# A planner's durations, attention weights turned by DMA planes, and the order of one layer's projections

## The chip, the core and the metric

The kernel runs on one core of a Trainium2 chip. The core has a matrix engine (TensorE, PE in the profile, with its weight loads as PEld), a vector engine (VectorE, DVE), a scalar engine (ScalarE, ACT), a general engine (GpSimd, POOL) and a queue engine (SyncE, SP) from which nearly all DMAs are issued. Each engine executes its own instructions in the order in which they were written; semaphores make one wait for another. PE writes only to PSUM, POOL cannot read PSUM. The metric is the device time of one execution in microseconds, lower is better.

## The reference

Two layers, each a mixer and a convolutional feed-forward block, over 272 valid tokens (16 learned ones and 256 of the input) of width 1024, in float32. What matters here:

```python
def mixer(hn, ...):
    proj = hn @ w_in                          # rq rk rv rg | hq hf hi hg | dq dk dv | m0 m1 m2
    o_ret = retention(rq, rk, rv, rg)         # 4 heads
    o_hg  = hgrn2(hq, hf, hi, hg)             # 8 heads, gated linear recurrence
    o_da  = diff_attention(dq, dk, dv)        # 8 heads
    y = sum(sigmoid(m_n) * (o_n @ w_branch[n]) for n, o_n in enumerate((o_ret, o_hg, o_da)))
    return y @ w_out

def diff_attention(q, k, v, lam_p, ...):      # per head: two score maps of 64 features
    p = softmax(where(allowed, q @ k.T, MASK))
    w = p[:, :, 0] - lam * p[:, :, 1]         # the attention weights
    return rms(w @ v) * subln_g * (1 - lambda_init)

def conv_ffn(hn, ...):                        # 1024 -> 5632, three-tap convolution, silu(gate) * val, -> 1024
```

Each layer normalises its input before the mixer and before the feed-forward block, and a final normalisation ends the model.

## The kernel before

**Products.** Everything is held with features on the partitions and tokens along the free axis. Every projection is made of 128x128 weight tiles; float32 accuracy comes from splitting both operands into a rounded part and a remainder, and adding three matmuls for each tile (lines 915 to 917: high weight with high input, high with low, low with high). Weights arrive in chunks of eight tiles (`_Weights.next`, line 626): a DMA on SP into `wraw` (3 buffers), a rounding copy on ACT into `whi`, a subtraction on DVE into `wlo` (4 buffers each). These are the "main" matmuls. A pair of output tiles `(name, j)` has 16 weight tiles, 48 main matmuls.

**Stages.** `ORDER` (lines 63 to 85) is the sequence of pairs in a layer, with marks between them: `+x` makes the side work of a branch (retention `ret`, recurrence `hga`/`hgb` and its outputs `hgoa`/`hgob`, attention halves `daa`/`dab` of four heads each), `!x` says by when it is due, and `*bn` splits the finished branch n into high and low tiles for its projection `bn`. Then `wo`, 22 pairs of `fi` and the second feed-forward product `fo` follow.

**The planner.** `_Plan` collects all instructions with their operands, dependencies, buffers and a cost in microseconds, and a key, the time at which each is wanted on a clock that the main matmuls' costs advance. `_Plan.order` (line 454) then simulates the five engines: on each it takes the instruction that can start first, and among those the one with the smallest key (`rank`, line 495); a change of engine costs `CROSS` 0.4 us, a freed buffer `FREE` 0.5 us, a change of ACT's tables `SWITCH` 1.3 us, and a DMA 2.0 us beyond its cost. The order found is written out as each engine's program. The costs come from `_Engine.__getattr__` (line 580): a fixed part and a part per element for each engine, with a few exceptions by operation. Line 905 gives the cost of the three main matmuls of a tile.

**Side work in turn.** `behind` (line 1360) makes a job of a head. `in_turn` keeps the order in which the instructions of a job take buffers of one kind, and `plan.queue(ops[0], mine[-1 - apart][-1])` lets a job start only when the last instruction of the job `apart` + 1 places before it is done; for attention `apart` is 2, retention 2, otherwise 1. Buffers are few: two PSUM banks each for `main`, `bank` and `acc`, 13 `slot` tiles, four `vsrc` tiles, two each of `wts`, `two_a` and `two_b`.

**An attention head.** `da_head` (line 1274) makes the scores `ds` of both maps on PE (line 1291) in two `bank` tiles, adds the mask and takes the maxima on DVE, exponentials on ACT, and combines both maps into `w` (tile `two_a`, tokens on the partitions) with multiplications on DVE. `turn` (line 1315) then turns three 128x128 blocks of `w` by PE transposes into a third `bank` tile `wt` (line 1317), and two ACT copies bring them to `a1` (tile `wts`). POOL copies two strips of 16 columns of `w` to `dt` for `da_tail`. The product with the values, `do`, is two PE matmuls, followed by a normalisation with a POOL all-reduce (`inverse`, line 974).

**Turned values.** The values of all branches need tokens on the partitions. `to_tokens` (line 951) turns them without PE: POOL copies the lower and the upper 16 bits of the float32 words into two planes (`apart`), a DMA transpose on SP turns each (`turned`), and POOL puts them together again (`vt`).

**The folded norm.** The first four pairs behind a normalisation multiply PSUM by `rstd`; for the fifth and later ones `Norm.next` has POOL multiply `y = h * rstd`, which ACT and DVE split into `xh` and `xl`.

## Time and profile before

| what | before |
|---|---|
| three runs, us | 1304.24, 1306.25, 1305.88 (median 1305.88) |
| the profiled execution, us | 1305.7 |
| its span from first to last instruction, us | 1303.9 |
| granted TensorE clock, mean | 0.998 |
| busy: PE, DVE, ACT, POOL, us | 1285.8, 986.7, 786.7, 270.3 |
| DMA transposes | 48 |

The span is what the trace covers; the execution's own time has 1.8 us more around it. In the lines of the profile, `out<-in` names the tiles that an instruction writes and reads, `xN` how often it occurs, and the figures behind a bar are busy us, mean ns of one, and idle us of the engine before it with what ended that idleness. Line 607 is the planner's common call, so most instructions are told apart by their tiles and not by their lines. SPq is the queue part of SP; a wait is written as "who, for which tile, behind whom: us in total, times, longest".

### The profile page before, as it was taken

To read this page: it belongs to the slowest core of one execution; us is meant where nothing else is said; L and a number is where in the kernel's file an instruction comes from. 1 tells how busy PE (TensorE), PEld (TensorE's weight loads), DVE (VectorE), ACT (ScalarE), POOL (GpSimd) and SP (SyncE) were. 2 spreads that over 40 slices of the span, in tenths; PEclk is the share of its full clock that TensorE was granted. 3 is DMA by queue.
4 is the path that set the end of the run, shared out by engine and by line. 5 is a ranking of instruction groups with operands and counts; after the bars stand their busy time and mean duration, and the time that the engine had idled before them with its cause. 6 is when DMAs were issued, how large, how long until landed. Compare 5 with 4: busy or idle time off the path is not lost.

```text
span 1303.9 us, 28637 instructions
## 1 busy us (share of the span) xinstructions
PE 1285.8 (99%) x11678; PEld 1256.7 (96%) x11678; DVE 986.7 (76%) x1589; ACT 786.7 (60%) x1282; POOL 270.3 (21%) x300
## 2 busy tenths in 40 slices
PE   9999999999999999999999999999999999999998
PEld 9999989999999999999999999899999999999986
DVE  7685897798686789886575768877986867898843
ACT  6746444746576567666456474447466765776643
POOL 5021262423422020000030212634223220200000
PEclk9999999999999999999999999999999999999999
DMA  7664665643744545555555646655446446466653
GB/s 272 200 179 147 173 178 155 164 160 125 199 138 157 182 156 178 183 173 183 175 178 185 186 149 185 179 155 168 159 138 199 145 162 198 144 207 196 201 190 112
DMA packets 86868, 225.36 MB, mean 173 GB/s; under 512 B 32976, under 2 KB 33104, under 8 KB 86736
## 3 DMA queue, kind: packets, MB, share of 16 engines
q1 hardware_dynamic: 86448, 223.00, 55.3%
q8 instruction: 92, 1.51, 0.5%
q10 hardware_dynamic: 288, 0.52, 0.1%
q14 instruction: 40, 0.33, 0.1%
HBM read 216.16 MB, written 1.05 MB: 167 GB/s over the span
## 4 chain that ended last, share of the span: by engine, by line
PE 88%; DVE 9%; issue 1%; ACT 1%; DMA 0%; SPq 0%; DVEq 0%; ACTq 0%
PE main L915 26%; PE main L917 26%; PE main L916 25%; DVE wlo L607 2%; PE fo L1430 2%; PE fo L1431 2%; PE fo L1429 2%; DVE two_b L607 1%; DVE two_a L607 1%; PE lev L1107 1%; PE ds L1291 1%; PE ho L607 1%; PE ro L607 1%; PE do L607 1%; DVE two_c L607 1%
## 5 line engine op out<-in xcount | busy, mean ns | idle before, releaser
L915 PE MATMUL main<-xh,whi 128*128 128x272 f32 (+1 forms) x2368 | 682.6, 288 | 0.8 <-ACT whi L607 0.8
L917 PE MATMUL main<-xh,wlo 128*128 128x272 f32 (+1 forms) x2368 | 673.9, 285 | 1.3 <-DVE wlo L607 0.7
L916 PE MATMUL main<-xl,whi 128*128 128x272 f32 (+1 forms) x2368 | 673.3, 284 | 1.5 <-DVE xl L607 1.5
L607 DVE TENSOR_TENSOR wlo<-wraw,whi 128x1024 fp32r<-128x1024 f32 (+1 forms) x411 | 512.0, 1250 | 187.8 <-ACT whi L607 186.6
L607 ACT ACTIVATE whi<-wraw 128x1024 fp32r<-128x1024 f32 (+1 forms) x411 | 427.5, 1042 | 250.9 <-PE main L916 166.3
L917 PEld LDWEIGHTS main<-xh,wlo 128*128 128x128 f32 x2368 | 446.5, 189 | 3.1 <-DVE wlo L607 2.3
L916 PEld LDWEIGHTS main<-xl,whi 128*128 128x128 f32 x2368 | 446.6, 189 | 2.2 <-DVE xl L607 1.9
L915 PEld LDWEIGHTS main<-xh,whi 128*128 128x128 f32 x2368 | 446.7, 189 | 2.0 <-ACT whi L607 1.0
L607 POOL TENSOR_TENSOR y<-h,rstd 128x272 f32<-128x272 f32 x32 | 34.6, 1112 | 318.1 <-ACT rstd L607 318.1
L607 POOL PARTITION_ALL_REDUCE hr<-hsq x36 | 65.8, 1837 | 88.9 <-ACT hsq L607 85.9
L607 DVE SCALAR_TENSOR_TENSOR two_b<-main,small,two_b 128x256 f32<-128x256 f32 (+2 forms) x144 | 65.3, 487 | 24.4 <-ACT two_b L607 22.7
L607 POOL COPY apart<-vsrc 128x512 uint16<-128x512 uint16 x48 | 40.7, 867 | 145.2 <-ACT vsrc L607 145.0
L607 ACT ACTIVATE two_b<-main,small 128x272 f32<-128x272 f32 (+1 forms) x72 | 37.3, 566 | 23.8 <-PE main L917 22.7
L915 PE MATMUL main<-ghi,whi 128*128 128x272 f32 x176 | 51.0, 290 | 0.0
L916 PE MATMUL main<-glo,whi 128*128 128x272 f32 x176 | 50.6, 287 | 0.0
L917 PE MATMUL main<-ghi,wlo 128*128 128x272 f32 x176 | 50.3, 286 | 0.0
L607 POOL COPY vt<-turned 128x512 uint16<-128x512 uint16 x32 | 37.0, 1160 | 29.2 <-DMA turned<-apart 29.0
L915 PE MATMUL main<-b0hi,whi 128*128 128x272 f32 (+1 forms) x128 | 37.9, 296 | 0.0
L915 PE MATMUL main<-b1hi,whi 128*128 128x272 f32 (+1 forms) x128 | 37.8, 296 | 0.0
L915 PE MATMUL main<-yhi,whi 128*128 128x272 f32 (+1 forms) x128 | 36.4, 284 | 0.0
L917 PE MATMUL main<-b0hi,wlo 128*128 128x272 f32 (+1 forms) x128 | 36.4, 284 | 0.0
L917 PE MATMUL main<-yhi,wlo 128*128 128x272 f32 (+1 forms) x128 | 36.3, 284 | 0.0
(235 smaller groups left out, 1970.1 us busy)
## 6 DMA issues: line engine op xcount, KB each, us to landing
wraw<-in_w SPq DMA_DIRECT2D x402, 512.0 KB, 3.4
h<-in_h SPq DMA_DIRECT2D x4, 272.0 KB, 5.1
dec<-in_dec SPq DMA_DIRECT2D x2, 544.0 KB, 4.9
wraw<-in_w SPq DMA_DIRECT2D x4, 256.0 KB, 4.2
const<-in_const SPq DMA_DIRECT2D x1, 937.0 KB, 5.6
turned<-apart SPq DMA_TRANSPOSE x48, 4.0
gain<-in_gl SPq DMA_DIRECT2D x1, 512.0 KB, 5.1
out<-y ACTq DMA_DIRECT2D x2, 256.0 KB, 2.8
```

The costliest lines, as they stand in the source:

```text
L607: self.plan.add(self.name, lambda: f(*args, **kw), cost, outs, ins, args[2] if method == "activation" else None)
L915: nc.tensor.matmul(o, wh, hi, start=first, stop=False)
L916: nc.tensor.matmul(o, wh, lo, start=False, stop=False)
L917: nc.tensor.matmul(o, wl, hi, start=False, stop=last)
L1107: nc.tensor.matmul(o, keys, x, start=True, stop=True)
L1291: nc.tensor.matmul(ss[m][:, at : at + nk], q[half, hd, q0 : q0 + P], k[half, hd, :nk], start=True, stop=True)
L1429: nc.tensor.matmul(o, gh, wh, start=False, stop=False)
L1430: nc.tensor.matmul(o, gl, wh, start=False, stop=False)
L1431: nc.tensor.matmul(o, gh, wl, start=False, stop=end)
```

## The change

Four things change.

1. **The planner's durations.** The fixed parts of ACT and DVE become 0.2 and 0.145 us (from 0.094 and 0.068), the three main matmuls of 272 columns 0.370 us (from 0.349), and scalars, shuffles, POOL adds, POOL copies, all-reduces and DMA transposes get costs of their own. POOL is given a state: when an all-reduce follows an add or multiply of two tensors or the other way round, `RELOAD`, 8 us, is booked.
2. **The turn of the attention weights.** In `da_head` the PE transposes and the two ACT copies are replaced by the way of `to_tokens`: per head four POOL copies into `apart` (256 and 128 columns for each of the two planes), two DMA transposes of 384 columns on SP, and two POOL copies into `a1`. Their tiles come from the same four `vsrc` buffers. The helpers `planes` and `halves` move out of `to_tokens` for this.
3. **The order.** The pairs of `b0` move behind `dk` and `dv` of the second half and behind the mark `+dab`. `*b0` stays where it was.
4. **The chain of heads.** A job can start when the job before the last has done its n-th instruction from the end: for `da_head` n is 8, its last `do` matmul, otherwise 1 as before.

```diff
-    + _pairs("dq", 2, 4) + _pairs("b0", 0, 4) + _pairs("dk", 2, 4) + _pairs("dv", 2, 4)
+    + _pairs("dq", 2, 4) + _pairs("dk", 2, 4) + _pairs("dv", 2, 4)
     + [("+dab", 0)]
-    + _pairs("m1", 0, 4)
+    + _pairs("b0", 0, 4) + _pairs("m1", 0, 4)
...
+    RELOAD = 8.0
...
+            if e == "pool" and op.func is not None:
+                if op.func != code:
+                    code, t = op.func, max(t, engines[e] + self.RELOAD)
             engines[e] = t + cost
...
+            kind = args[2] if method == "activation" else None
             if self.name == "act":
                 cost += 0.093 * (len(aps) - 2) - (0.043 if ins[0].tensor.name in self.plan.psum else 0.0)
-            elif self.name == "pool" and method != "memset":
-                cost += 1.6e-3 * n
-            if method == "partition_all_reduce":
-                cost = 0.4 + 5.4e-3 * n
-            if method == "reciprocal":
+            elif method == "tensor_scalar":
+                cost += 0.065 * (len(aps) - 2) - 0.14
+            elif method in ("scalar_tensor_tensor", "stream_shuffle", "tensor_tensor_reduce"):
+                cost += 0.06
+            elif method == "reciprocal":
                 cost += 7 * self.each * n
-            elif method == "tensor_tensor_scan":
-                cost += self.each * n
+            elif self.name == "pool" and method == "tensor_tensor":
+                cost, kind = 0.55 + 2.1e-3 * n, method
+            elif self.name == "pool" and method == "tensor_copy":
+                cost = 0.35 + 1.0e-3 * n
+            elif method == "partition_all_reduce":
+                cost, kind = 0.2 + 6.3e-3 * n, method
...
             elif method == "dma_start":
-                cost = self.fixed + self.each * n * outs[0].shape[0]
+                cost = self.fixed + self.each * n * outs[0].shape[0] + (0.7 if kw.get("transpose") else 0.0)
...
-    act = _Engine(plan, nc.scalar, "act", 0.094, 0.833e-3)
-    dve = _Engine(plan, nc.vector, "dve", 0.068, 1.042e-3)
+    act = _Engine(plan, nc.scalar, "act", 0.2, 0.833e-3)
+    dve = _Engine(plan, nc.vector, "dve", 0.145, 1.052e-3)
...
-        cost = 3 * ((T - t0) / 2400 + 0.003)
+        cost = 3 * ((T - t0) / 2400 + 0.01)
...
+    def planes(name, n):
+        return new(tp, [P, 4 * T], U16, "vsrc", 4, name)[:, : 2 * n].rearrange("p (i x) -> p i x", i=2)
+
+    def halves(t):
+        return t.bitcast(U16).rearrange("p (x two) -> p x two", two=2)
...
             w = sb[0]
-            wt = bank("wt")
-
-            def turn(wt=wt, w=w):
-                for i, c in enumerate((0, P, T)):
-                    nc.tensor.transpose(wt[:, i * P : (i + 1) * P], w[:, c : c + P], ident)
-
-            plan.add("pe", turn, 0.33, [wt[:, : 3 * P]], [w[:, : T + P]])
-            act.activation(a1[:, META + P : T + P], wt[:, : 2 * P], AF.Copy)
-            act.activation(a1[:, META : META + P], wt[:, 2 * P : 3 * P], AF.Copy)
+            apart, turned = planes("apart", 3 * P), planes("turned", 3 * P)
+            for i in range(2):
+                for c, n, at in ((0, 2 * P, P), (T, P, 0)):
+                    pool.tensor_copy(apart[:, i, at : at + n], halves(w[:, c : c + n])[:, :, i])
+            for i in range(2):
+                sync.dma_start(turned[:, i].rearrange("p (b x) -> p b x", x=P), apart[:, i], transpose=True)
+            for i in range(2):
+                pool.tensor_copy(halves(a1[:, META : T + P])[:, :, i], turned[:, i])
...
-        def behind(f, until, apart=1):
+        def behind(f, until, apart=1, after=1):
...
-            mine.append(ops)
+            mine.append((ops, after))
             if len(mine) > apart:
-                plan.queue(ops[0], mine[-1 - apart][-1])
+                before, which = mine[-1 - apart]
+                plan.queue(ops[0], before[-which])
...
-            cost = 3 * (BANK / 2400 + 0.012)
+            cost = 3 * (BANK / 2400 + 0.0133)
...
                 for hd in range(4):
-                    behind(lambda: da_head(b, hd), "da", 2)
+                    behind(lambda: da_head(b, hd), "da", 2, 8)
```

More of the change, by code (lines that the diff above doesn't have):

```diff
@@ L470, in order @@
         count = 0
-        tables = "le"
+        tables, code = "le", "tensor_tensor"
         beside = False
@@ L605, in call @@
             elif method == "dma_start":
-                cost = self.fixed + self.each * n * outs[0].shape[0]
-            self.plan.add(self.name, lambda: f(*args, **kw), cost, outs, ins, args[2] if method == "activation" else None)
+                cost = self.fixed + self.each * n * outs[0].shape[0] + (0.7 if kw.get("transpose") else 0.0)
+            self.plan.add(self.name, lambda: f(*args, **kw), cost, outs, ins, kind)
         return call
@@ L949, in split @@
         tt(lo, x, hi.bitcast(F32), SUB)
+    def planes(name, n):
+        return new(tp, [P, 4 * T], U16, "vsrc", 4, name)[:, : 2 * n].rearrange("p (i x) -> p i x", i=2)
+    def halves(t):
+        return t.bitcast(U16).rearrange("p (x two) -> p x two", two=2)
     def to_tokens(src, vt, e):
-        def planes(name):
-            return new(tp, [P, 4 * T], U16, "vsrc", 4, name)[:, : 8 * P].rearrange("p (i x) -> p i x", i=2)
-        apart, turned = planes("apart"), planes("turned")
-        halves = lambda t, i: t.bitcast(U16).rearrange("p a (x two) -> p a x two", two=2)[:, :, :, i]
+        apart, turned = planes("apart", 4 * P), planes("turned", 4 * P)
         for i in range(2):
             pool.tensor_copy(apart[:, i].rearrange("p (c f x) -> p c f x", c=2, f=2),
-                             halves(src[:, :, : 2 * P], i).rearrange("p f (c x) -> p c f x", c=2))
+                             halves(src.rearrange("p f t -> p (f t)"))[:, :, i].rearrange("p (f t) -> p f t", f=2)[:, :, : 2 * P].rearrange("p f (c x) -> p c f x", c=2))
         for i in range(2):
@@ L963, in to_tokens @@
         for i in range(2):
-            pool.tensor_copy(halves(vt[:, :, e : e + 2 * P], i), turned[:, i].rearrange("p (c x) -> p c x", c=2))
+            pool.tensor_copy(vt.bitcast(U16).rearrange("p c (x two) -> p c x two", two=2)[:, :, e : e + 2 * P, i], turned[:, i].rearrange("p (c x) -> p c x", c=2))
     def tail_tokens(tails):
```

2 lines of the change are left out of this document (removed).

## The prediction

> **What bounds the kernel now.** I read the page's busy shares first, then the chain that ended last, the groups of instructions on TensorE, the waits of TensorE, and a table of busy time by stretch for the attention stages.
>
> ```profile
> span 1303.9 us, 28637 instructions
> ...
> PE 1285.8 (99%) x11678; PEld 1256.7 (96%) x11678; DVE 986.7 (76%) x1589; ACT 786.7 (60%) x1282; POOL 270.3 (21%) x300
> ...
> PE 88%; DVE 9%; issue 1%; ACT 1%; DMA 0%; SPq 0%; DVEq 0%; ACTq 0%
> ```
>
> TensorE (PE) is busy 1285.8 of 1303.9 us, and the chain that ends last is 88% PE. No stage waits for weights for long. So the time moves only by what PE no longer executes, and by the small waits at which its in-order queue stands still for another engine. The waits that the profile names, longest first:
>
> ```profile
> PE lev L1107 <- DVE hf L607: 3.2, 2, 1.7
> PE main L916 <- DVE xl L607: 1.5, 2, 1.1
> PE ho L607 <- DVE ho L607: 1.4, 2, 0.8
> PE wt L1317 <- DVE two_a L607: 1.1, 3, 0.5
> ...
> PE main L917 <- DVE wlo L607: 0.7, 3, 0.3
> PE lev L1107 <- DVE tot L607: 0.4, 1, 0.4
> PE lev L1107 <- DVE hq L607: 0.4, 1, 0.4
> ...
> PE lev L1107 <- ACT qt L607: 0.3, 1, 0.3
> ```
>
> Each is a place where the planner put a PE instruction earlier than its input was ready. Which engine is tight there is read from the stretches (columns: stretch, its length, then busy us and instruction count of PE, PEld, DVE, ACT, POOL, then the granted clock, DMA share and GB/s):
>
> ```profile
> 244.00:264.00 20.00, 20.00 (x165) 20.00 (x164) 16.26 (x19) 14.57 (x24) 15.74 (x17) 1.00 0.70 176
> 264.00:284.00 20.00, 19.19 (x156) 19.00 (x155) 19.72 (x37) 8.58 (x15) 4.15 (x3) 1.00 0.43 138
> ...
> 362.00:384.00 22.00, 22.00 (x176) 20.97 (x174) 17.91 (x43) 18.55 (x41) 8.71 (x10) 1.00 0.43 143
> ...
> 915.00:935.00 20.00, 19.43 (x164) 19.23 (x163) 19.79 (x37) 9.33 (x17) 4.28 (x4) 1.00 0.44 135
> ```
>
> DVE is at 19.72 of 20 us where the first attention half starts in layer 0 (19.79 in layer 1), and PE loses 0.8 and 0.6 us there; POOL has room in the attention stretches (4.15 of 20, 8.71 of 22) but not beside the value blocks (15.74 of 20).
>
> **Part 1, the turn leaves PE.** Each of 16 `da_head` calls (4 heads, two halves, two layers) loses three PE transposes and two ACT copies. What one turn costs PE is read from the starts around it:
>
> ```profile
> 294.04 0.28 PE L916 MATMUL main<-b0lo,whi 128*128 128x272 f32 x1
> 294.16 0.29 PE L917 MATMUL main<-b0hi,wlo 128*128 128x272 f32 x1
> 294.29 0.49 PE L1317 MATMUL wt<-const,two_a 128*128 128x128 f32 x3
> 294.54 0.37 PE L915 MATMUL main<-b0hi,whi 128*128 128x272 f32 x1
> 294.75 0.29 PE L916 MATMUL main<-b0lo,whi 128*128 128x272 f32 x1
> ...
> 296.49 0.84 PE L607 MATMUL do<-wts,vt 128*128 128x272 f32 x4
> ```
>
> Main matmuls start 0.12 us apart (294.04 to 294.16). Across the turn it is 0.38 (294.16 to 294.54), and the first one behind it takes 0.21 instead of 0.12: 0.26 + 0.09 = 0.35 us. Times 16: **-5.6 us**, all of it on the path. The bounds are -5.0, if two turns that now adjoin other side work save no switch, and -5.6.
>
> The turn's waits go with it:
>
> ```profile
> L1317 PE MATMUL wt<-const,two_a 128*128 128x128 f32 x48 | 8.9, 278 | 1.3 <-DVE two_a L607 1.1
> ...
> L1317 PEld LDWEIGHTS wt<-const,two_a 128*128 128x128 f32 x48 | 5.9, 140 | 2.5 <-DVE two_a L607 2.5
> ```
>
> The matmul row shows 1.3 us of idleness, the weight loads that come first 2.5; a wait under the 0.28 us of a pipelined matmul hides in busy time, so the two bound it from 1.3 to 3.8. I take **-2.5**, the loads' row, since it is the load that needs the weights `w`. The two ACT copies of a head go too:
>
> ```profile
> L607 ACT ACTIVATE wts<-wt x32: 258/332/403, 295.3 to 1045.3; 128x256 f32<-128x256 f32 x16, 128x128 f32<-128x128 f32 x16
> ```
>
> 32 x 0.33 = 10.6 us of an engine at 60%, behind no PE wait of the list: 0. If ACT had been late there, they would be part of the turn-to-`do` way below, which is replaced as a whole.
>
> **Part 2, the planes.** What takes the turn's place is, per head, four POOL copies (256 and 128 columns, twice), two DMA transposes of 384 columns on the SP queue, two POOL copies back. The turn-to-`do` way was 2.2 us (294.29 to 296.49). The nearest rows are the value blocks, which do the same at 512 columns:
>
> ```profile
> L607 POOL COPY apart<-vsrc x48: 611/626/1680, 74.0 to 991.6; 128x512 uint16<-128x512 uint16 x48
> ```
>
> ```profile
> L607 SPq DMA_TRANSPOSE turned<-apart x48: 1194/1197/2137, 74.7 to 993.2; - x48
> L607 POOL COPY vt<-turned x32: 767/938/1912, 77.2 to 998.1; 128x512 uint16<-128x512 uint16 x32
> ...
> DMA to landing us min/median/max: 2.4/4.0/6.0
> ```
>
> ```profile
> L607 POOL COPY apart<-vsrc 128x512 uint16<-128x512 uint16 x48 | 40.7, 867 | 145.2 <-ACT vsrc L607 145.0
> ```
>
> By columns alone the copies take 0.3 and 0.2 us when nothing is in their way, and the copies back 0.6; the page's mean of `apart`, 867 ns against the minimum of 611, adds about 0.26 each. That is 2.3 to 3.9 us of POOL per head, 37 to 62 us in all, on an engine busy 270.3 us: no bound by itself.
>
> What counts is whether `do`, the next PE instruction of the head, comes later than planned. Let S be the end of the head's last DVE multiply-add. In the new plan POOL books 0.35 us + 1 ns a column (0.61, 0.48), a transpose 1.31 us of SP and 2.0 us to land, a copy back 0.73, and every change of engine 0.4. The four copies end at S + 1.8, the second transpose follows the first at S + 3.05, lands for POOL at S + 6.75, and `do` is due at S + 7.9. On the chip, from the rows: the copies end at S + 0.45 to 1.3; the second transpose goes out 1.2 to 2.1 us behind the first (its own time on SP) and lands 4.0 us later, at S + 5.7 to 7.4; copied back in 0.6 to 0.9, S + 6.3 to 8.3. With the slowest landing (6.0) the middle of that, 7.3, becomes 9.3. A crossing costs far less than 0.4, which is what pays for this:
>
> ```profile
> 293.19 0.37 DVE L607 SCALAR_TENSOR_TENSOR two_a<-two_a,dm,two_b 128x144 f32<-128x144 f32 x1
> ...
> 293.62 0.20 POOL L607 COPY dt<-two_a 128x16 f32<-128x16 f32 x1 [0.41 <-DVE two_a L607]
> ```
>
> (293.56 to 293.62, 0.06 us.) So in the middle `do` is early by 0.6, and in the tail late by 1.4 us. Bounds: 0, and 16 x 1.4 = 22.4 us if every head is in the tail. I take **+3**, a quarter of the heads late by about 0.8, because the median landing is nearer to the early end. While PE waits at `do`, main matmuls queue behind it, so such a wait is paid in full. A POOL copy back that waits for its landing holds the other head's all-reduce behind it, and so its normalisation, for which only `b2` waits, much later.
>
> The two extra SP instructions of a head (1.2 us each, 32 in all) stand ahead of weight loads, and so does their wait for POOL. The cover is that weights are ready early: ACT's splits wait for PE to free a buffer, and SP itself for DVE.
>
> ```profile
> L607 ACT ACTIVATE whi<-wraw 128x1024 fp32r<-128x1024 f32 (+1 forms) x411 | 427.5, 1042 | 250.9 <-PE main L916 166.3
> ```
>
> ```profile
> SPq L607 <- DVE wlo L607: 695.8, 270, 6.8
> ```
>
> I cost it at 0; without that cover it is 1.2 us a transpose, 38 us at most.
>
> The added POOL copies also stop DVE, in the same rows' terms:
>
> ```profile
> L607 DVE SCALAR_TENSOR_TENSOR two_a<-two_a,dm,two_b x32: 367/501/1245, 292.4 to 1043.4; 128x272 f32<-128x272 f32 x16, 128x144 f32<-128x144 f32 x16
> ```
>
> ```profile
> 298.18 1.78 POOL L607 PARTITION_ALL_REDUCE hr<-hsq  x1
> 298.18 1.24 DVE L607 SCALAR_TENSOR_TENSOR two_a<-two_a,dm,two_b 128x144 f32<-128x144 f32 x1
> ```
>
> The 144-column multiply-add takes 0.37 us alone and 1.24 beside a POOL instruction that started with it. This lateness is inside the tail above.
>
> **Part 3, the planner's durations.** They change the written order everywhere. Old and new against the rows: a weight split on ACT 0.95 to 1.05 (trace 1.042); the DVE one 1.135 to 1.22; three main matmuls 0.349 to 0.370 (trace: 3 x 0.12 to 0.124).
>
> ```profile
> L607 DVE TENSOR_TENSOR wlo<-wraw,whi x411: 418/1224/2232, 6.0 to 1288.0; 128x1024 fp32r<-128x1024 f32 x132, 128x512 fp32r<-128x512 f32 x4, 128x256 fp32r<-128x256 f32 x1
> ```
>
> A plan that knows how long DVE takes puts `lev` and `ho` behind some more main work. Those rows bound the gain: 3.2 + 1.4, with the smaller `lev` waits (0.4, 0.4, 0.3) 5.7 us. As a plan can also move waits to new places, the loss is bounded by the same 5.7. I take half of the gain, **-2.8**: longer durations only make a planned start later, not a real one.
>
> One new duration does not fit: 8 us when POOL changes between its add/multiply code and the all-reduce.
>
> ```profile
> 474.15 8.46 POOL L607 TENSOR_TENSOR y<-h,rstd 128x272 f32<-128x272 f32 x8 [66.64 <-ACT rstd L607]
> ```
>
> ```profile
> 473.63 0.43 ACT L607 ACTIVATE rstd<-rstd 128x272 f32<-128x272 f32 x1
> ...
> 478.30 1.33 ACT L607 ACTIVATE xh<-y,small 128x272 fp32r<-128x272 f32 x3
> ```
>
> The first multiply after the reduces starts 0.09 us after its input, eight take 8.46 us, and ACT reads results 4 us on: no 8 us anywhere. The Trainium skill, "GPSIMD Engine Reference", section Instruction dispatch, says that the first call of freshly loaded code pays about 6 us with no visible instruction; this trace shows none at that change, and by the skill's figure the 8 us booked at each of the two feed-forward starts would be nearly right and this term 0. By the trace the planner delays `y`, and what reads it, in its order without need. The `xl` waits above (1.5 us in two places) lie at that point; I take **+0.5**, between 0 and +3 (twice the present waits).
>
> **Part 4, the order.** `dq`, `dk`, `dv` of the second half move ahead of `b0` (four pairs). PE's work stays the same; b0's inputs get more time, and its split tiles stay in their slots longer. Six pairs with rotations and value copies now follow each other where DVE already stands at 19.72 of 20; I take **+1**, bounds -1.4 (the 0.8 and 0.6 us of those stretches gone, as second-half heads now spread into `b0`) and +3. The relaxed chain, by which a head starts when the head two before it has done its `do`, removes no PE work: 0; it covers the longer head.
>
> **Sum.** -5.6 - 2.5 + 3 - 2.8 + 0.5 + 1 = -6.4 us. The profiled execution took 1305.7 us (the span and 1.8 us around it), so 1299.3; the three runs' median is 1305.88, 0.2 above, so **1299.5**. 0.2%, 2.6 us, is about what a measurement of this kernel can tell from no change.
>
> **Rivals.** *The planes are late (slower).* Place: `do` of every head. The mechanism is the tail of part 2: slow landings, copies held by DVE. With every head 1.4 us late: 22.4 - 5.6 - 2.5 = +14.3, 1320. It decides from a mean wait of (5.6 + 2.5) / 16 = 0.5 us a head. For it speaks the spread of landings (2.4 to 6.0) and 1680 ns against 611 for a copy; against it the 0.34 us of slack at each crossing, and that no row has PE waiting for `vt`. The Trainium skill speaks for it too: "VectorE: DVE Perf Modes", Rules for kernel authors, says to transpose 128x128 on TensorE where PSUM will do, and by DMA otherwise; this trace agrees on the latency alone (0.49 against 4.0 us).
> *The waits only move.* Half a us at each `do` eats parts 1 and 2 (16 x 0.5 = 8): 1305.9, no change. For it: the same plan gave the turn its waits.
> *The plan gains more.* `do` never waits and `lev`, `ho` neither: -5.6 - 2.5 - 5.7 = -13.8, 1292. For it: all those waits are DVE lateness of under 2 us; against it: DVE at 19.72 of 20 stays.
>
> **Chances.** Forecast 0.48 (own range 1295 to 1303), the better plan 0.16, waits only move 0.16, late planes 0.20 (1309 to 1320). Faster by over 0.2%: 0.48 + 0.16 = 0.64; within: 0.16; slower: 0.20. The range 1290 to 1313 leaves out the far end of the late planes and of the better plan, under 2 in 10.
>
> **What would show it.** No `wt<-const,two_a` rows; 80 `turned<-apart` transposes; POOL at 307 to 332 us. Right: PE waits at `do` for POOL `wts` of about 3 us in total, `lev` waits under 3.2. The late planes show as that `do` wait above 8 us; a wrong part 4 as `main` waiting for `wlo` or a rotation right behind the first `dk`; a wrong part 3 as new waits at `xl`.

## The result, and the profile after

The changed kernel takes 1310.3 us (median of 6 runs, 1309.33 to 1312.26) against 1306.07 for the kernel before (6 runs, 1304.24 to 1307.39): a ratio of 1.0034, with a 95% interval of 1.0021 to 1.0047. It is slower by 4.2 us. The prediction was 1299.5 us and faster; the time lies inside the range, on the wrong side of no change.

The profiled execution took 1309.37 us, 1307.6 of them its span. First the busy shares and the chain that ended last, of the kernel after:

```profile
span 1307.6 us, 28633 instructions
...
PE 1282.4 (98%) x11630; PEld 1252.3 (96%) x11630; DVE 983.6 (75%) x1589; ACT 775.8 (59%) x1248; POOL 325.0 (25%) x396
...
PE 80%; DVE 11%; POOL 3%; DMA 2%; issue 2%; ACT 1%; SPq 0%; DVEq 0%; ACTq 0%; POOLq 0%
```

TensorE has 48 matmul instructions fewer and is busy 3.4 us less, POOL 54.7 us more. The span is nevertheless longer by 3.7 us, so TensorE stands still more: 25.2 us of the span instead of 18.1. The chain that ended last now runs through POOL (3%) and the DMAs (2%), where before it had 0% for the DMAs and no POOL. Where TensorE stands, in the list of its waits (total us, times, longest):

```profile
PE lev L1116 <- DVE hf L614: 4.8, 4, 1.5
PE main L923 <- DVE xl L614: 3.1, 4, 1.2
PE do L614 <- POOL wts L614: 2.8, 3, 1.4
PE vm L614 <- POOL tails L614: 1.9, 2, 1.3
PE main L924 <- DVE wlo L614: 1.6, 4, 1.0
PE main L924 <- DVE wts L614: 1.5, 1, 1.5
PE wt L614 <- POOL dt L614: 1.0, 1, 1.0
...
PE ho L614 <- DVE ho L614: 0.5, 1, 0.5
```

The turn's waits are gone, as is the turn, and `ho` is down from 1.4 to 0.5. But `lev` rose from 3.2 to 4.8, `xl` from 1.5 to 3.1, `wlo` from 0.7 to 1.6, and `do`, `vm` and `dt`, all behind POOL, are new to the list's upper part. The same stretches as before the change (stretch, length, busy us and count of PE, PEld, DVE, ACT, POOL, granted clock, DMA share, GB/s):

```profile
244.00:264.00 20.00, 18.75 (x150) 18.38 (x149) 15.45 (x20) 15.25 (x22) 13.51 (x14) 1.00 0.56 148
264.00:284.00 20.00, 20.00 (x165) 20.00 (x165) 19.77 (x33) 10.99 (x18) 10.42 (x5) 1.00 0.45 148
362.00:384.00 22.00, 22.00 (x176) 21.20 (x176) 16.78 (x41) 17.89 (x33) 11.44 (x18) 1.00 0.48 139
915.00:935.00 20.00, 18.03 (x147) 17.44 (x146) 19.83 (x33) 10.21 (x18) 9.92 (x6) 1.00 0.28 89
```

VectorE is as full where the attention starts as it was (19.77 and 19.83 of 20 us). In layer 1 TensorE now loses 2.0 us of those 20, where it lost 0.6; in layer 0 it loses 1.25 just ahead of that stretch and nothing in it, where it lost nothing and 0.8.

A plain sum over the whole trace tells the same. The table is worked out from the start times of all TensorE matmuls. "Side work" is the time from the start of each matmul that is not a main one to the next start. A wait is what a main matmul takes to the next start beyond its pitch (0.1235 us at 272 columns and 0.117 at 258, about the middle of the measured steps), once where a main matmul follows and once where side work follows. The second feed-forward product is the same in both and left out. Waits in the middle of side work count as side work.

| TensorE, us | first to last matmul | side work | waits, main to main | waits, main to side |
|---|---|---|---|---|
| before | 1296.58 | 92.4 | 21.9 | 11.6 |
| after | 1300.25 | 86.0 | 26.3 | 17.2 |
| difference | +3.7 | -6.4 | +4.4 | +5.7 |

Side work fell by 6.4 us. In the kernel before, the 16 turns take 6.3 us from their first transpose to the next start: 0.24 or 0.25 each, and 2.4 us of waits inside five of them. The waits gave back 10.1.

### The profile page after: what moved, and what is told of

Read it like the earlier page. It is cut to its first block, busy times and chain, and to the rows that moved or that the text cites. A ratio compares the mean times of both kernels' runs of the same rounds, so it can differ in the third digit from the quotient of the medians.

```text
span 1307.6 us, 28633 instructions
## 1 busy us (share of the span) xinstructions
PE 1282.4 (98%) x11630; PEld 1252.3 (96%) x11630; DVE 983.6 (75%) x1589; ACT 775.8 (59%) x1248; POOL 325.0 (25%) x396
## 4 chain that ended last, share of the span: by engine, by line
PE 80%; DVE 11%; POOL 3%; DMA 2%; issue 2%; ACT 1%; SPq 0%; DVEq 0%; ACTq 0%; POOLq 0%
PE main L922 24%; PE main L923 23%; PE main L924 23%; DVE wlo L614 3%; PE fo L1439 2%; PE fo L1440 2%; PE fo L1438 2%; DVE two_b L614 1%; DMA wraw<-in_w 1%; DVE two_c L614 1%; PE lev L1116 1%; POOL apart L614 1%; PE ro L614 1%; DMA turned<-apart 1%; DVE two_a L614 1%
## 5 line engine op out<-in xcount | busy, mean ns | idle before, releaser
L614 POOL PARTITION_ALL_REDUCE hr<-hsq x36 | 71.7, 2009 | 94.0 <-ACT hsq L614 94.0
L614 POOL COPY apart<-two_a 128x256 uint16<-128x256 uint16 x64 | 34.1, 564 | 47.0 <-DVE two_a L614 46.9
```

The lines of the kernel that those rows point to most:

```text
L614: self.plan.add(self.name, lambda: f(*args, **kw), cost, outs, ins, kind)
```

## The experiments

Each time is compared with runs of the kernel before on the same chip, whose medians were 1305.3 to 1305.8 (1306.07 for the change itself); the ratio has its 95% interval. "d" is the median less the median before of the same group.

| kernel | median us | d us | ratio |
|---|---|---|---|
| the change | 1310.3 | +4.2 | 1.0034 (1.0021 to 1.0047) |
| before + durations | 1316.3 | +10.9 | 1.0085 (1.0072 to 1.0099) |
| before + planes | 1323.0 | +17.6 | 1.0136 (1.0122 to 1.0150) |
| change without durations | 1304.49 | -0.9 | 0.9996 (0.9987 to 1.0005) |
| change without planes | 1313.88 | +8.5 | 1.0067 (1.0054 to 1.0080) |
| change, `RELOAD` 0 | 1308.23 | +2.4 | 1.0020 (1.0011 to 1.0029) |
| change, old cost of main matmuls | 1312.56 | +6.7 | 1.0053 (1.0040 to 1.0067) |
| without durations, new cost of main matmuls | 1312.15 | +6.3 | 1.0049 (1.0036 to 1.0061) |
| before + order + chain | 1312.01 | +6.2 | 1.0047 (1.0034 to 1.0060) |
| before + order | 1307.04 | +1.7 | 1.0011 (1.0003 to 1.0020) |
| without durations, transposes booked longer | 1317.74 | +12.4 | 1.0094 (1.0081 to 1.0108) |
| before, `CROSS` 0.41 / 0.39 | 1305.37 / 1305.37 | +0.1 / -0.2 | 1.0001 (0.9992 to 1.0010) / 1.0004 (0.9994 to 1.0014) |
| without durations, `CROSS` 0.41 | 1304.81 | -0.7 | 0.9992 (0.9983 to 1.0001) |
| change, `CROSS` 0.41 | 1301.6 | -3.7 | 0.9973 (0.9961 to 0.9984) |
| change, `CROSS` 0.39 | 1309.99 | +4.5 | 1.0037 (1.0024 to 1.0049) |
| change, `FREE` 0.52 | 1305.28 | -0.3 | 0.9998 (0.9989 to 1.0007) |
| change, less VectorE work | 1300.81 | -4.5 | 0.9968 (0.9957 to 0.9980) |
| the same, `CROSS` 0.41 | 1300.19 | -5.2 | 0.9966 (0.9954 to 0.9979) |

### The parts by themselves

**The durations alone**: all new costs of part 3, nothing else.

```diff
-    act = _Engine(plan, nc.scalar, "act", 0.094, 0.833e-3)
-    dve = _Engine(plan, nc.vector, "dve", 0.068, 1.042e-3)
+    act = _Engine(plan, nc.scalar, "act", 0.2, 0.833e-3)
+    dve = _Engine(plan, nc.vector, "dve", 0.145, 1.052e-3)
...
-        cost = 3 * ((T - t0) / 2400 + 0.003)
+        cost = 3 * ((T - t0) / 2400 + 0.01)
```

> The kernel before with the planner's new durations alone (costs, the POOL state of 8 us, the main cost); the turn stays on PE, order and chain of heads stay. Theory D, the durations are the loss: their re-sorted plan adds the waits seen at xl, wlo and lev (3.1 + 1.6 + 4.8 us after, against 1.5 + 0.7 + 3.2 before), so 1309 to 1312 us here. Theory P, the planes are the loss through POOL and SP: 1302 to 1305 us here.

Measured: +10.9 us, more than either theory had. The edit leaves the work as it is (the number of ACT's table loads alone changes, from 31 to 29) and rewrites the order. Its longest waits, in the list of TensorE's waits:

```profile
PE vm L614 <- POOL tails L614: 6.4, 3, 2.7
PE lev L1114 <- DVE hf L614: 4.6, 3, 2.2
PE main L923 <- DVE xl L614: 2.7, 3, 1.2
```

A plan with durations that are for the most part closer to the trace gave a slower order than one with short ones. The waits at `lev` and `xl`, which it was to remove, grew (3.2 and 1.5 before), and `tails` is new.

**The planes alone**: the turn by DMA, with the old order, the old chain of heads and the old durations.

```diff
-            wt = bank("wt")
...
+            apart, turned = planes("apart", 3 * P), planes("turned", 3 * P)
...
+                sync.dma_start(turned[:, i].rearrange("p (b x) -> p b x", x=P), apart[:, i], transpose=True)
```

> The kernel before with the turn moved to the DMA planes alone; old durations, old order, old chain of heads. Theory D: PE loses 5.6 us of turns and 2.5 us of their waits and gains some 3 us of waits at do, so 1300 to 1303 us. Theory P: the transposes hold weight loads on SP and the copies hold tails and dt on POOL, so 1308 to 1312 us.

Measured: +17.6 us, the slowest of the parts. The waits of TensorE in this kernel:

```profile
PE main L915 <- ACT b2hi L607: 10.9, 2, 6.0
PE do L607 <- DVE tw L607: 4.7, 2, 3.2
```

Neither theory had this. TensorE hardly stands at `do` behind the planes (1.5 us in the same list). It stands once a layer at the projection `b2`, whose input is the finished attention. A head takes 16.5 to 27.1 us here from its first scores to its last `do` (10.5 to 13.4 in the kernel before), and with the old order and the old chain the last of them ends too late. The prediction named `b2` only as something that waits "much later".

**Without the durations**: the planes, the order and the chain, with the old costs.

```diff
-    RELOAD = 8.0
...
-    act = _Engine(plan, nc.scalar, "act", 0.2, 0.833e-3)
+    act = _Engine(plan, nc.scalar, "act", 0.094, 0.833e-3)
```

> The changed kernel with the old durations (no POOL state either): planes, order and chain of heads stay. Theory D: 1299 to 1303 us, faster than before. Theory P: 1309 to 1313 us, as the changed kernel or slower.

Measured: -0.9 us, no change that can be told, and between the two theories. Its one long wait is that for the planes:

```profile
PE do L607 <- POOL wts L607: 7.0, 5, 2.2
```

So the new chain and order together take away what the planes alone cost at `b2`, and on top of that the durations are worth +4.2 + 0.9 = +5.1 us in this order. Taken the other way round, with the durations first (+10.9), order and chain bring 8.5 - 10.9 = -2.4 (the next kernel's 8.5) and the planes -4.3.

**Without the planes**: order, durations and chain, with the turn on TensorE.

```diff
-            apart, turned = planes("apart", 3 * P), planes("turned", 3 * P)
...
+            wt = bank("wt")
+            plan.add("pe", turn, 0.33, [wt[:, : 3 * P]], [w[:, : T + P]])
```

> The changed kernel with the turn back on PE: new durations, order and chain of heads stay. Theory D: the durations' loss without the planes' gain, 1312 to 1318 us. Theory P: 1301 to 1305 us.

Measured: +8.5 us. The planes are worth 4.2 - 8.5 = -4.3 us beside the new durations.

### Which duration, and which part of the order

**No reload state.**

```diff
-    RELOAD = 8.0
+    RELOAD = 0.0
```

> The changed kernel with the POOL state's 8 us set to 0, all else as changed. Theory R, the 8 us that the trace does not show are the loss: 1304 to 1306 us, with xl waits back from 3.1 to about 1.5 us. Theories M and E (below: main cost, engine durations): 1309 to 1312 us.

Measured: +2.4 instead of +4.2, between the two theories, and the `xl` waits are 2.7 us, not the 1.5 of theory R. So 1.8 us is what goes with the 8 us in this one order; the scatter found below is larger. The trace of the changed kernel has nothing that answers to the 8 us. These are the rows on ACT and POOL at the first feed-forward block:

```profile
477.40 0.43 ACT L614 ACTIVATE rstd<-rstd 128x272 f32<-128x272 f32 x1
```

```profile
477.92 8.74 POOL L614 TENSOR_TENSOR y<-h,rstd 128x272 f32<-128x272 f32 x8 [60.72 <-ACT rstd L614]
```

The multiply starts 0.09 us after `rstd` is there (477.83 to 477.92), behind all-reduces, as it did before (POOL had been idle for 60.72 us). The Trainium skill, "GPSIMD Engine Reference", section Instruction dispatch, has the first call of freshly loaded code pay about 6 us; no run here shows it at this change of code.

**The old cost of main matmuls in the new plan, and the new cost in the old one.**

```diff
-        cost = 3 * ((T - t0) / 2400 + 0.01)
+        cost = 3 * ((T - t0) / 2400 + 0.003)
```

> The changed kernel with three main matmuls booked at 0.349 us again (0.370 in the changed one), all other new durations kept. Theory M: the old figure made the planned PE run 6% ahead of the real one, so that splits and side work were written earlier than needed, a lead that hid lateness; without it the plan is just in time. Then 1303 to 1306 us here, with main-matmul waits on xl and wlo down by 3 us or more. Theory E, the engines' new durations are the loss: 1309 to 1312 us.

> The changed kernel with the old durations of all engines and no POOL state, but three main matmuls booked at 0.370 us. Theory M: 1308 to 1312 us, as the changed kernel. Theory E: 1303 to 1306 us, as with all durations old (1304.5).

Measured: +6.7 and +6.3, both slower than what they started from (+4.2 and -0.9). The first speaks for theory E, the second for theory M. With TensorE planned fast beside slow engines, the weights come too late by the list of waits:

```profile
PE main L924 <- DVE wlo L614: 5.8, 10, 1.3
PE main L923 <- DVE xl L614: 4.0, 5, 1.8
```

With TensorE planned slow beside fast engines, it is the attention weights:

```profile
PE do L607 <- POOL wts L607: 10.3, 9, 2.4
```

Either mixture is slower than both whole sets, so nothing here points to the main cost as the one bad number among the durations. The differences between the mixtures and the changed kernel (2 us) are again within the scatter found below.

**Order and chain without planes and durations**, and **the order alone**. Their diffs to the kernel before:

```diff
-    + _pairs("dq", 2, 4) + _pairs("b0", 0, 4) + _pairs("dk", 2, 4) + _pairs("dv", 2, 4)
+    + _pairs("dq", 2, 4) + _pairs("dk", 2, 4) + _pairs("dv", 2, 4)
...
-    + _pairs("m1", 0, 4)
+    + _pairs("b0", 0, 4) + _pairs("m1", 0, 4)
```

```diff
-                    behind(lambda: da_head(b, hd), "da", 2)
+                    behind(lambda: da_head(b, hd), "da", 2, 8)
```

> The kernel before with the new order and the relaxed chain of heads alone: the turn on PE, old durations. Against the run with the planes added (1304.5 us) it gives what the planes are worth in this order. If they give the 5.6 us of turns and lose what PE waits at do (7.0 us there) less the turn's waits (2.5 us): 1305.6 us, planes worth about 1 us. If the order itself costs (theory O: six pairs of rotations and value copies together), 1308 us or more, and the planes are worth 4 us or more.

> The kernel before with the new order alone (b0 behind the second half's projections), turn on PE, old durations, old chain. Order and chain together took 1312.0 us. Theory O, the order is the cost (rotations and value copies of six pairs together): 1310 to 1313 us. Theory C, the relaxed chain is (heads closer together, so their PE work finds DVE late): 1304 to 1307 us.

Measured: the order alone +1.7 (just past the range of theory C), both +6.2, so the chain that heads may start earlier adds +4.5 where nothing needs it. (A head waits for the head two before it; `apart` 2 counts these places.) In the kernel with both, TensorE's turn waits more than before (1.1 us for `two_a` there):

```profile
PE wt L1317 <- DVE dm L607: 2.8, 4, 1.2
PE wt L1317 <- DVE two_a L607: 1.2, 4, 0.5
```

The planes take away the turn that waits there, and are worth -0.9 - 6.2 = -7.1 us on this base. The parts of the change do not add up from their effects alone: the planes cost 17.6 us without the order and the chain and gain 7.1 with both.

Which of the two the planes need was not run (planes and order with the old chain). The order has a share by the traces. It puts the four pairs of `b0`, 192 main matmuls or some 24 us, between the start of the second half's heads and `b2`. With the order alone the scores of these heads start at 354.8, 359.3, 377.3 and 382.1 us in layer 0, where the kernel before has 365.2, 368.6, 384.0 and 387.3. The chain brings the last two further forward, to 368.9 and 377.4.

### A longer booking for the transposes

The way from a head's `w` to its `do` is longer than planned (below). So the kernel without durations got 1.5 us more for each transpose.

```diff
-                cost = self.fixed + self.each * n * outs[0].shape[0]
+                cost = self.fixed + self.each * n * outs[0].shape[0] + (1.5 if kw.get("transpose") else 0.0)
```

> Planes, order and chain with the old durations (1304.5 us; PE waited 7.0 us at do for the planes), and 1.5 us more booked for each DMA transpose. Theory B, the wait at do is only a booking that is too short, since PE has main work to do meanwhile: the do wait falls below 3 us and the time to 1298 to 1302 us. Theory S: the do wait falls, other waits take its place, 1303 to 1308 us.

Measured: +12.4 us against -0.9 without it, outside both theories. It did what it was for: the wait at `do` fell from 7.0 us (kernel without durations) to 0.9. But the heads end later, and the deadline at `b2` is missed in one layer; weights are late as well:

```profile
PE main L915 <- ACT b2hi L607: 5.9, 1, 5.9
PE main L917 <- DVE wlo L607: 5.9, 10, 1.3
```

A longer booking is no gain by itself: the wait at `do` went, and waits at `b2` and for the weights that are larger together took its place. Nor is the booking right in itself. For 384 columns it has 4.1 us from issue to landing where the old costs have 2.6, and this kernel's trace shows 3.2 in the median; 2.1 of the 4.1 are booked as the queue's own time, which is 1.2 in the trace.

### Is it the values, or only the order that they happen to give?

All those edits change the written order in many places. To see what an order change without any meaning does, a constant of the planner was moved by a hair, in the kernel before and in the changed one (and in the one without durations). Told by their tiles and shapes in the traces, it moves 55 of TensorE's matmuls in the kernel before and 147 in the changed one.

```diff
-    CROSS = 0.4
+    CROSS = 0.41
```

> The kernel before with one planner constant, the cost of a change of engine, at 0.41 instead of 0.40 us: no work changes, some 120 PE instructions change places. Theory S, a planned order is one draw of a scatter of several us, and the kernel before lies at its good end: 1308 to 1312 us. Theory N, only the parts of the change matter: 1304.5 to 1307 us.

> The changed kernel with the same constant at 0.41: some 390 PE instructions change places. Theory S: anywhere from 1304 to 1314 us, away from 1310 by 2 us or more as likely as not. Theory N: 1309 to 1312 us.

Measured: nothing in the kernel before (+0.1), and -3.7 in the changed one, which was +4.2: 0.01 us in the planner's cost of a crossing is worth 7.9 us of device time, more than any single term of the prediction's sum. This version, 1301.6 us, beats both kernels, and is below the range that theory S had for it. Two readings were left: a trend with the constant (L in the expectations), or a draw. So `CROSS` went to the other side and another constant was moved, with the controls.

```diff
-    CROSS = 0.4
+    CROSS = 0.39
```

```diff
-    FREE = 0.5
+    FREE = 0.52
```

> The changed kernel with the cost of a change of engine at 0.39 instead of 0.40 us (0.41 took 1301.6 us). Theory S, the time of the changed kernel is one draw of a scatter, decided in the stretches where DVE is full: 1301 to 1312 us, no trend from 0.39 over 0.40 to 0.41. Theory L, the smaller or larger booking itself does it (a longer crossing is closer to what the planes need): 0.39 is slower than 0.40, 1310 to 1315 us.

> The changed kernel with the time of a freed buffer at 0.52 instead of 0.50 us; the crossing at 0.40. Theory S: 1301 to 1312 us, and with the other draws a mean near 1306. Theory L has nothing to say here but no change: 1309 to 1312 us.

> The kernel before with the crossing at 0.39 us. At 0.41 it stayed at 1305.4 us. Theory S for the changed kernel alone (its DVE is full for longer): 1304 to 1307 us here. If the kernel before scatters as well: 2 us or more away from 1305.4.

> Planes, order and chain with old durations, the crossing at 0.41 us (0.40 took 1304.5 us). Theory S: 1300 to 1312 us. If the old durations are the better ones by themselves: 1303 to 1306 us.

Measured: the change with 0.39 stays at +4.5, with `FREE` 0.52 it is at -0.3 (single runs from 1301.65 to 1306.99). The kernel before does not move (-0.2), nor does the one without durations (-0.7 against -0.9). A trend does not account for `FREE`. The changed kernel's time has a scatter that the others did not show: +4.2, +4.5, -0.3 and -3.7 for four nearly equal planners. Their mean is +1.2, and the kernel without durations has -0.8 from two. That the others stay still may have a plain reason: the same nudges move fewer of their matmuls (55 and 36 in the kernel before, 66 in the one without durations, against 147, 82 and 104 in the changed one). This was not separated. All parts above that were measured on the new durations rest on one draw each, so a difference of a few us between them is not shown to be the part's own.

Where the draws differ is seen in one stretch, the start of the attention in layer 1. First the kernel before, then the changed one, then the changed one with `CROSS` 0.41 (columns as above):

```profile
905.00:970.00 65.00, 64.19 (x525) 62.22 (x524) 57.79 (x126) 38.34 (x90) 21.20 (x27) 1.00 0.51 156
```

```profile
905.00:970.00 65.00, 61.75 (x496) 59.59 (x495) 57.65 (x119) 35.43 (x72) 34.98 (x46) 1.00 0.54 163
...
930.00:940.00 10.00, 8.50 (x70) 8.28 (x69) 9.90 (x21) 3.83 (x6) 0.77 (x1) 1.00 0.43 151
```

```profile
905.00:970.00 65.00, 64.28 (x527) 62.96 (x526) 59.50 (x119) 34.27 (x70) 34.52 (x47) 1.00 0.55 165
...
930.00:940.00 10.00, 10.00 (x83) 9.64 (x83) 9.90 (x22) 3.85 (x6) 1.20 (x2) 1.00 0.49 165
```

In the same 65 us the changed kernel has 31 matmuls fewer than its sibling. At about 0.125 us each that is 3.9 us, half of the 7.8 us between the two spans (1307.6 and 1299.8). Counted by work and not by time, the 600 main matmuls from the 6601st on (907.7 to 996.4 us in the changed kernel) take 88.7 us in the changed kernel and 88.3 with `CROSS` 0.39, but 83.3 with `CROSS` 0.41 and 85.3 in the profiled run of `FREE` 0.52 (1301.65 us, its fastest). So 5.3 of the 7.8 us arise here. From 930 to 940 VectorE is busy 9.90 us in both: it is not more work, but which of its operations comes first. What happened there can be read line by line in the changed kernel, on VectorE and on TensorE:

```profile
931.88 0.69 DVE L614 TENSOR_TENSOR dq<-dq,two_c 128x516 f32<-128x516 f32 x1
...
932.63 1.22 DVE L614 TENSOR_TENSOR wlo<-wraw,whi 128x1024 fp32r<-128x1024 f32 x1
```

```profile
933.91 0.39 PE L924 MATMUL main<-xh,wlo 128*128 128x272 f32 x1 [1.50 <-DVE wts L614]
```

The low part of the weights, `wlo`, stands on VectorE behind a rotation of `dq` (and a small operation), and the matmul that reads it starts at 933.91, 0.06 us after the split ends (932.63 + 1.22 = 933.85), after 1.50 us of idleness. (The list of waits files it under `wts`, a small operation that ends then as well.) With `CROSS` 0.39 TensorE stands for 1.47 us at the same matmul, the 6771st main one; with `CROSS` 0.41 and `FREE` 0.52 it does not stand there. If a full VectorE is what makes the order matter (V in the expectations), less work on it should make it matter less.

**Less VectorE work**: the sine product of the rotation of `dq` and `dk`, and its addition, are left out.

```diff
-        tt(sh, sh, pair(const[:, (2 * table + 1) * T + t0 : (2 * table + 2) * T]), MUL)
-        tt(out, out, sh, ADD)
+        if table == 0:
+            tt(sh, sh, pair(const[:, (2 * table + 1) * T + t0 : (2 * table + 2) * T]), MUL)
+            tt(out, out, sh, ADD)
```

> The changed kernel without the second half of the rotation of dq and dk (the sine product and its addition are left out, two DVE operations of about 0.7 us for each of 16 pairs, 22 us of DVE in all, most of it in the stretches around the start of the attention). Theory V, the full DVE in those stretches turns small differences of the order into waits: 1297 to 1303 us, PE busy at least 64 of 65 us from 905 to 970. If DVE there is not the reason: 1308 to 1311 us.

> The same with the cost of a change of engine at 0.41 us. Theory V: within 2.5 us of the run before, since DVE has room in both. If the scatter comes from elsewhere: 4 us or more between the two, as between 1310.3 and 1301.6.

Measured: 1300.81 and 1300.19 us. The two `CROSS` values, 8.7 us apart in the full kernel (1310.3 and 1301.6), are now 0.6 apart. TensorE's 63.99 of 65 us is at the edge of what theory V asked. The same stretches in the first of them:

```profile
905.00:970.00 65.00, 63.99 (x522) 62.18 (x521) 52.55 (x113) 35.22 (x76) 35.91 (x51) 1.00 0.59 172
930.00:940.00 10.00, 10.00 (x82) 9.64 (x81) 7.83 (x19) 4.07 (x7) 1.19 (x2) 1.00 0.57 194
```

VectorE has room (7.83 of 10), and TensorE loses nothing from 930 to 940. That supports the reading that the attention's start is bound by VectorE as tightly as by TensorE, and that the order decides which waits. It does not prove it for all of the scatter: it is one pair of orders, and another pair (0.39 and 0.40) was as equal with a full VectorE; the edit itself also reorders everything, and it was not made in the kernel before, so its gain is no measure of the loss.

## Why the prediction was wrong

**Part 1, the turn leaves TensorE: right.** No `wt<-const,two_a` row is left. Of the 8.1 us taken for the turn and its waits, the kernel before has 7.7: 6.3 of side work, of which 2.4 are waits (2.5 foretold), and 16 times 0.09 for the slower first matmul behind it. Side work fell by 6.4.

**Part 2, the planes: the size near, by luck; the way mis-timed.** POOL is busy 325.0 us (307 to 332 foretold), and the wait at `do` is 2.8 us (3 foretold). That match is luck: the same wait is 7.0 in the kernel without durations and 0.9 with `CROSS` 0.41. The transposes are where they should be; the rows of the tile `apart` after:

```profile
L614 SPq DMA_TRANSPOSE turned<-apart x80: 1179/1202/2666, 77.5 to 1047.6; - x80
L614 POOL COPY apart<-two_a x64: 287/400/1388, 299.4 to 1045.2; 128x256 uint16<-128x256 uint16 x32, 128x128 uint16<-128x128 uint16 x32
...
DMA to landing us min/median/max: 2.3/3.6/6.5
```

The time from the end of `w` (S) to the second copy back was foretold as 6.3 to 8.3 us. Over the 16 heads it is 9.0 to 17.9, median 11.0. The first head, on POOL in order of time:

```profile
299.37 0.40 POOL L614 COPY apart<-two_a 128x256 uint16<-128x256 uint16 x1 [8.45 <-DVE two_a L614]
300.00 0.87 POOL L614 COPY apart<-two_a 128x128 uint16<-128x128 uint16 x3 [0.22 <-DVE two_a L614]
...
302.68 0.88 POOL L614 COPY wts<-turned 128x384 uint16<-128x384 uint16 x1 [1.53 <-DMA turned<-apart]
305.05 0.67 POOL L614 COPY apart<-vsrc 128x512 uint16<-128x512 uint16 x1 [1.50 <-ACT vsrc L614]
...
307.76 1.61 POOL L614 COPY apart<-vsrc 128x512 uint16<-128x512 uint16 x1
309.32 1.20 POOL L614 COPY tails<-vsrc 128x32 f32<-128x32 f32 x1
310.46 0.60 POOL L614 COPY wts<-turned 128x384 uint16<-128x384 uint16 x1
```

The second plane is copied back at 310.46. Its transpose goes out at 301.58, 1.26 us behind the first (300.32), and even by the slowest landing above, 6.5 us, its data was there at 308.1. The copy stands in POOL's order behind value copies and `tails` of other work. I had summed a head's own instructions and allowed for slow landings, not for what POOL has in between. The wait at `do` stayed small because the written order has `do` late too, 10.6 to 17.9 us after S, with main work before it. The price came out elsewhere: heads this long need the earlier start, or they miss `b2` (+17.6 us for the planes alone, 10.9 of it named as a wait at `b2`). That deadline was in none of my rivals.

On the worth of the turn itself: the Trainium skill, "VectorE: DVE Perf Modes", Rules for kernel authors, prefers TensorE for a 128x128 transpose where PSUM will do. In this kernel, with TensorE busy 98% of the span, the way by DMA was worth 4.3 and 7.1 us on the two bases where the heads start early, and cost 17.6 where they do not. Which way wins thus hung on whether the heads had room for the longer way.

**Part 3, the durations: the step that failed.** "I take half of the gain, -2.8: longer durations only make a planned start later, not a real one." With the +0.5 of the reload state the prediction had -2.3. Measured: +10.9 alone and +5.1 on the rest. The `lev` waits rose from 3.2 to 4.8 us, and `xl` from 1.5 to 3.1, the prediction's own sign of a wrong part 3. The bound of plus 5.7 was worked out from the waits that existed, but a new order makes waits at places that had none (`tails` 6.4 us in the kernel with the durations alone).

One such place is the same in every draw. The first main matmuls behind the first folded norm, the hundred from the 201st on, take 12.34 us in the kernel before. In all ten kernels here with the old engine durations it is 12.33 or 12.34; in all ten with the new ones it is 13.08 to 13.88 (13.83 in the changed kernel). There TensorE waits for the low part of the normalised input, which VectorE splits off too late:

```profile
35.81 0.39 PE L923 MATMUL main<-xl,whi 128*128 128x272 f32 x1 [0.40 <-DVE xl L614]
...
37.36 0.39 PE L923 MATMUL main<-xl,whi 128*128 128x272 f32 x1 [0.53 <-DVE xl L614]
```

The loss stays with `RELOAD` 0 (13.88) and with the old main cost (13.08), and is not there with the new main cost alone (12.33), so it comes with the new durations of the other operations. That is 0.7 to 1.5 us. Most of the rest arises at the start of the attention in layer 1: up to the 6601st main matmul the profiled runs with and without durations are level (907.7 and 907.8 us), at the 7201st the changed kernel is 3.1 us behind. But the draws differ just there, by 5.3 us between the slowest and the fastest. By their means (+1.2 with the durations, -0.8 without) the durations cost about 2 us and not 5.1, from four values that lie 8 us apart. How much they cost on average, and which duration does it, stays open.

**Part 4, the order and the chain: half wrong.** The order alone was to cost +1 and cost +1.7. The relaxed chain was set at 0, since it "removes no PE work". It is +4.5 without the planes, where the heads stand closer together and their turns wait 4.0 us by the list of waits (2.0 with the order alone); the rest of the 4.5 is not named there. This is the other step that failed, a term put at nothing. With the planes, the order and the chain together keep `b2` from waiting; the two were a condition of part 2, and I costed them as if they were separate.

**The sum.** From part to part, each on top of those before: order +1.7, chain +4.5, planes -7.1, durations +5.1, together +4.2. The prediction had +1, 0, -5.1 (parts 1 and 2) and -2.3, together -6.4. The planes came out 2 us better than foretold; the 10.6 us that are missing, and those 2, lie in what an order does to waits: +0.7, +4.5 and +7.4. Most of these kernels were run in one draw, and another sequence of the parts splits the same 4.2 otherwise (+10.9, -2.4, -4.3 above).

**The rivals.** "The planes are late" gave 1320 by waits at `do` above 8 us; the time fell on its side, its mechanism, `do` standing for the planes, did not occur (2.8 us). "The waits only move" had the mechanism nearest to the truth, but had them move only to `do`, and only as much as was gained. The "better plan" at 1292 never came; the best draw of the change, 1301.6, is still 2.1 us above the point forecast.

## What to carry to other kernels

In a kernel whose order a planner writes and whose main engine is busy 98% of the span, a change of any cost is also a new draw of the order: before a few us are put down to a change, move a constant by a hair, in both kernels, and see how far each time moves. A step that is made longer has its deadline where its result is needed, not only at its next instruction, so count what else stands in the same engine's order and cost the edit that starts it earlier together with it. If a second engine is full in one stretch (19.8 of 20 us here), look there first for what an order costs; durations closer to the trace did not help here.

## What the runs showed that was not expected

- Booking more for a step that takes longer than planned can make the order worse: 1.5 us more for a transpose made the kernel 13 us slower (1304.49 to 1317.74).
- How far the time hangs on the order differs between kernels that do nearly the same work: 1305.3 to 1305.5 us with three values of `CROSS` in the kernel before, 1301.6 to 1310.3 in the changed one.
- The same 11630 matmuls are busy 1282.4 us in the changed kernel and 1278.3 with `CROSS` 0.41, whose page has the row below: the spans differ by 7.8 us, but the idle time of TensorE (25.2 and 21.5 us) by 3.7. Some of TensorE's standing still is inside its busy time, so idle time alone understates what waits cost.

```profile
PE 1278.3 (98%) x11630; PEld 1249.7 (96%) x11630; DVE 983.9 (76%) x1589; ACT 775.1 (60%) x1248; POOL 328.4 (25%) x396
```

- With 80 transposes instead of 48 on the same queue the landing did not get longer: 3.6 us in the median, before 4.0 (the added ones have 384 columns, the others 512).
